# A three-layer block in split float32: all low parts subtracted on VectorE, none on GpSimd

## The chip, the cores and the metric

The kernel runs on one core of one Trainium2 chip. A core has five engines with instruction queues of their own: TensorE (PE, with weight loads shown apart as PEld), VectorE (DVE), ScalarE (ACT), GpSimd (POOL) and SyncE (SP), which here only issues transfers. The metric is the device time of one execution in microseconds (us); less is better.

## What is computed

512 tokens of 1024 features go through a first block and then a second one of two layers. Cut to what matters here:

```
first block:  h = x + mixing(norm(x))                 # state space, gated mixing, w_out
              h = h + experts(norm(h))                # 8 heads; each token picks 16 of 16384 experts per head:
                                                      #   sum over them of gate * gelu(norm(h) . U[e]) * V[e]
              h = h + sigmoid(norm(h) w_gate) * (p w_proj);  then a norm
second block: h = [16 meta tokens, h]
              layer 0: h += mixer_ab(norm(h));  h += relu(norm(h) w_ff1)^2 w_ff2
              layer 1: h += attention(norm(h)); h += relu(norm(h) w_ff1)^2 w_ff2
```

All of it is float32.

## The kernel before

A large product is made in three passes of the type float32r. Each operand is written as a high and a low part: `split` copies the source to the high part on ScalarE (line 288, which rounds to float32r) and then subtracts this from the source to give the low part (line 289). The passes are high by high, high by low and low by high (`product`, line 314); the pass with the low part of the weights comes last.

`weights` fetches one unit of 128 x 1024 weights, 512 KB, from HBM into a buffer `w_raw` by a transfer on SP's queue and splits it into `w_hi` and `w_lo`, of which there are two buffers each. `w_raw` has six buffers in the experts' part and two or three elsewhere. A unit feeds 24 matmuls, 16 with `w_hi` and 8 with `w_lo`. The argument `eng` of both functions names the engine that subtracts: VectorE where it is not given, GpSimd where it is.

The stages in order of time, with the place of GpSimd's subtractions:

- 0 to 280 us: `mix_layer`, with state space, gates and `w_out`. Six units of `w_in`, and two of `wq` at the start of `peer`.
- 280 to 300 us: the norm of the experts' input. For eight chunks of features, `hn` is split; the odd four on GpSimd.
- 300 to 600 us: `retrieve` searches the best experts of all tokens: per head, products with `wq` and with keys, then on VectorE `max`, `max_index` and `match_replace` (lines 1091 to 1095), and comparisons with the sums of pairs (lines 1147 to 1154). Beside it, `ahead` makes products of units of `U` that are needed later (70 in all, here and in the next stage), and keeps their gelu in HBM. Nearly all units are subtracted on GpSimd.
- 600 to 840 us: `scatter_gates` makes one-hot tiles of the chosen experts by comparisons on VectorE (line 1216), scales half of one on GpSimd (line 1217) and half on ScalarE, and multiplies them on TensorE into a table of gates. The other products of `ahead` go beside it, subtracted on GpSimd.
- to 1690 us: the dense experts, for the first 384 tokens. For each of 16 groups of 8 keys: the rest of the `U` products, gates times gelu (line 949), their split `ga`, and 8 products with units of `V` added to h (line 984). Here `less_loaded` chose VectorE or GpSimd for each unit by an account of the load of both, with 1.13 us for VectorE and 2.3 us (`W_POOL`) for GpSimd; `pace` adds to it what the row work costs.
- Beside the last three: `Own` gathers, for the last 128 tokens, rows of `U` and `V` by indirect transfers that GpSimd issues (line 1058), one row of 4 KB for each token at a time; VectorE multiplies each (line 1037) or adds it (line 1041). Four are under way at a time.
- 1690 to 1830 us: `per_layer`, then `delta_inputs` of the second block, whose twelve units of `w_ab` are subtracted on GpSimd.
- After 1830 us: the rest of the second block. VectorE makes all subtractions.

The order of instructions on each engine is not written out by hand: the framework plans it before the run from a timeline that it simulates (`schedule_with_timeline_sim=True`), starting from the order of the program. On the chip each engine takes its instructions in that order.

Of the kernel before, what the change touches and what calls it, by code (L numbers as in the profile page):

```python
# [11 lines left out]
F32 = mybir.dt.float32  # L12
# [34 lines left out]
def _rows(v):  # L47
    """A vector laid out along the free axis of all 128 partitions."""
    return _c(np.broadcast_to(np.asarray(v).reshape(1, -1), (128, np.asarray(v).size)))


def _feat(x):
    """[tokens, features] -> [128, chunks, tokens]."""
    return _c(x.T.reshape(-1, 128, x.shape[0]).transpose(1, 0, 2))


def _pairs(b):
    """[32 groups, 64 states, 16 channels] -> block diagonal over pairs of groups [128, 16, 32]."""
    out = np.zeros((2, 64, 16, 2, 16), b.dtype)
    b = b.reshape(16, 2, 64, 16)  # L60
    for g in range(2):
        out[g, :, :, g, :] = b[:, g].transpose(1, 0, 2)
    return out.reshape(128, 512)
# [10 lines left out]
def _half_cols(w):  # L74
    """The two members of every rotary pair into two halves of a head."""
# [110 lines left out]
class Ctx:  # L186
    """Pools and constants; tokens are `T` columns in `nb` PSUM banks of `hn` each."""
# [9 lines left out]
    def enter(self, name, side):  # L197
        """A pool that `leave` closes; once h is on the right, the sides are exchanged."""
# [13 lines left out]
    def psum(self, mm, aux):  # L212
        """PSUM as `mm` accumulators of all tokens and `aux` single banks."""
# [5 lines left out]
    def raw_units(self, n):  # L219
        """`n` buffers for units of weights, in an order that all that is loaded there keeps."""  # L220
# [5 lines left out]
    def work(self):  # L226
        """Pools of small tiles and of the tiles of norms."""
# [20 lines left out]
def newton_rsqrt(c, v, n):  # L248
    """1/sqrt(v) of a [128, n] tile, elementwise, to float32 accuracy."""
# [13 lines left out]
def exp_exact(c, out, x, n):  # L263
    """exp of a [128, n] tile to float32 accuracy."""
# [19 lines left out]
def split(c, src, hi, lo, scale=None, eng=None):  # L284
    """src (times a per-partition scale) as a sum of two float32r parts."""
    nc = c.nc
    if scale is None:
        nc.scalar.activation(hi, src, AF.Copy)  # L288
        (eng or nc.vector).tensor_tensor(lo, src, hi.bitcast(F32), ALU.subtract)  # L289
# [5 lines left out]
def weights(c, src, nk, n, eng=None):  # L295
    """Load one unit of weights and split it: two float32r views [128, nk, n]."""
# [5 lines left out]
    split(c, raw, hi, lo, eng=eng)  # L302
# [3 lines left out]
def product(c, ps, parts, first=True, last=True, n=None, late=1):  # L306
    """ps [M, nb, 512] += sum of stationary^T moving over three passes; moving holds all tokens (or one bank of n).
    The passes with the second part of the stationary (late=1) or moving (late=2) side come last."""
# [9 lines left out]
def token_stats(c, acc, width):  # L318
    """rsqrt(mean + eps) per token from partial sums acc [128, T]: [tokens of a tile, tiles]."""
# [15 lines left out]
def along_tokens(c, col):  # L335
    """A per-token column [128, tiles] as a row on all partitions: PSUM banks of `hn` tokens."""
# [15 lines left out]
def square_sum(c, acc, k, src, eng=None, scale=1.0):  # L352
    """acc += (src * scale) squared (the first chunk starts it)."""
# [9 lines left out]
def token_rows(c, acc, width, name):  # L363
    """rsqrt(mean + eps) as rows on all partitions, in SBUF, and as columns."""
# [4 lines left out]
def column_rows(c, col, name):  # L369
    """A per-token column as rows in SBUF."""  # L370
# [7 lines left out]
class Rows:  # L378
    """The rows of a norm, made when first asked for; uses of them wait until `hold` products are under way."""
# [20 lines left out]
class S5:  # L400
    """Powers of the discretised transition, the input and output weights of chunks of 4 tokens."""
# [74 lines left out]
    def scaled(self, dst, src, by, eng, name):  # L476
        """dst = src * by; parts along the second axis, `by` the real and the imaginary part and the negative of that."""
# [9 lines left out]
    def inputs(self, j):  # L487
        """The input weights of position j in a chunk; position 3 comes first."""
# [9 lines left out]
    def transposes(self):  # L498
        """The input weights as the stationary side of products."""
# [10 lines left out]
    def rotations(self, k):  # L510
        """The rotations of positions 2^k and more, after those before, of a chunk."""
# [11 lines left out]
    def powers(self):  # L523
        """The output weights of the state."""
# [17 lines left out]
    def inside(self, q):  # L542
        """The output weights of the chunk itself, of 4 pairs of groups."""
# [16 lines left out]
def s5_states(c, pool, xs, S, hf):  # L560
    """The states before each chunk, of 8 of the 16 pairs of groups; xs is [(position in chunk, channel), pair, chunk]."""
# [38 lines left out]
def s5_outputs(c, pool, xs, S, hf, h, ys):  # L600
    """ys = gelu of the outputs of these pairs."""
# [21 lines left out]
def mix_layer(c):  # L623
    """Block 1 up to the residual after w_out, which becomes c.h."""
    nc, d = c.nc, c.d
    tt = nc.vector.tensor_tensor
    with c.pool("mix", "right") as pool:
# [3 lines left out]
        with c.pool("s5", "right") as s5p:  # L631
# [3 lines left out]
            with c.pool("s5t", "right") as tmp:  # L635
                S = S5(c, s5p, outer, tmp)
                acc = c.norm("acc")
                for k in range(8):
                    x = pool.tile([128, 512], F32, name="u", bufs=5)
                    nc.sync.dma_start(x, d["xT"][:, k])  # L640
                    if k == 0:
                        w = weights(c, d["w_in"][0], 8, 128, eng=nc.gpsimd)
# [7 lines left out]
                for m in range(4):  # L650
                    ps = c.mm()
                    product(c, ps, [((w[0][:, k], w[1][:, k]), xk[k]) for k in range(8)])
                    if m < 3:
                        w = weights(c, d["w_in"][m + 1], 8, 128, eng=None if m else nc.gpsimd)
# [16 lines left out]
                for what, step in [(o[0], int(o[1])) for o in V_ORDER]:  # L671
                    if what == "v":
# [9 lines left out]
                        else:  # L682
                            w = weights(c, d["w_in"][4], 8, 128, eng=nc.gpsimd)
# [12 lines left out]
            for what, step in [(o[0], int(o[1])) for o in U_ORDER]:  # L696
                if what == "u":
                    ps = c.mm()
                    product(c, ps, [((w[0][:, k], w[1][:, k]), xk[k]) for k in range(8)])
                    if step < 3:  # L700
                        w = weights(c, d["w_in"][5 + step], 8, 128, eng=nc.gpsimd)
# [26 lines left out]
            def half(m, k0, pair):  # L728
                """Half of the product of output chunk m; weights come for two chunks at a time."""
# [60 lines left out]
def sgu_norm(c, vn, mean):  # L790
    """The norm of v [token, head, tile, channel] in place, from its sums over channels."""
# [14 lines left out]
def sgu_weights(c, pool):  # L806
    """The causal weights of the mixing, and what it adds."""
# [14 lines left out]
def sgu_mix(c, gp, u, vn, wb):  # L822
    """u *= causal mixing of the normalised v."""
# [21 lines left out]
PER_CALL = 0.6  # L845
# [6 lines left out]
PER_USE = 1.2  # L852
PER_FETCH = 1.04
W_POOL = 2.3


def peer(c, acc, hn):
    """Its norm goes to hn, and h += the retrieved experts, summed with their gates: all experts with the gates of the first 384 tokens,
    and for the last 128 tokens the rows of their own experts."""
# [3 lines left out]
    with c.pool_d("peer_d") as dram, c.pool("gel", "left") as gelp:  # L863
        rows = Own(c, gelp)
        w_q = [weights(c, d["wq"][k], 8, 128, eng=nc.gpsimd) for k in range(2)]
# [14 lines left out]
        for k in range(8):  # L880
            t = gelp.tile([128, 512], F32, name="gel", bufs=GEL)
            nc.vector.scalar_tensor_tensor(t, c.h[k], c.vec("g_ffn", k), row, op0=ALU.mult, op1=ALU.mult)
            split(c, t, hn[0][:, k], hn[1][:, k], eng=nc.gpsimd if k % 2 else None)
# [7 lines left out]
        def reach(a, eng):  # L891
            """gelu of the dense tokens against the 128 experts of key a: [expert, token]."""
            w = weights(c, d["U"][a], 8, 128, eng=eng)
# [6 lines left out]
        def ahead(k, eng):  # L900
            for _ in range(min(k, len(first) - len(early))):
                s = first[len(early)]
                early[s] = dram.tile([128, n], F32, name="early%d" % s)
                nc.sync.dma_start(early[s], reach(s, eng))

        place = lambda: gelp.tile([128, 512], F32, name="gel", bufs=GEL)
        load = [0.0, 0.0]

        def less_loaded():
            """The engine that ends a split of weights first."""  # L910
            k = 0 if load[0] + 1.13 <= load[1] + W_POOL else 1
            load[k] += (1.13, W_POOL)[k]
            return (nc.vector, nc.gpsimd)[k]

        with c.pool("sel", "right") as sel:
# [9 lines left out]
            def beside(i, n):  # L925
                ahead((i + 1) * rest // n - i * rest // n, nc.gpsimd)
# [4 lines left out]
        ahead(128, nc.gpsimd)  # L931

        with c.pool("ga", "right") as gp:
# [4 lines left out]
            def prepare(s, ga):  # L938
# [3 lines left out]
                else:  # L942
                    gel = reach(s, less_loaded())
# [14 lines left out]
            def pace(cost):  # L958
                """Rows in step with the work done, out by the last group."""
# [4 lines left out]
                load[0] += PER_USE * k + PER_CALL  # L964
                load[1] += PER_FETCH * k

# [3 lines left out]
            for g in range(16):  # L970
                if g < 15:
                    nxt = pair()
                for m in range(8):
# [5 lines left out]
                    w = weights(c, d["V"][8 * g + m], 8, 128, eng=less_loaded())  # L979
# [17 lines left out]
class Own:  # L997
    """The last 128 tokens, one per partition: rows of their experts, gathered in step with other work."""
# [19 lines left out]
    def choose(self, e16):  # L1018
        """The experts [128, 2, 16] of the next two heads."""
# [4 lines left out]
    def use(self, i, r, at=None):  # L1024
        """Row i times its weight, which passes through `at` of the work that this keeps step with."""
# [17 lines left out]
    def go(self, k, place):  # L1043
        """Fetch the next k rows; their numbers pass through a tile of the work that they keep step with."""
# [18 lines left out]
    def add(self):  # L1063
        """The rest of the rows; then their sum into h."""
# [13 lines left out]
def retrieve(c, tk, hk, rows, go, ahead, first):  # L1078
    """The experts and gates of all tokens, [token, tile, head, slot]; two heads at a time, with other work between.
    `first` holds products of the tokens before their norm, with its rows."""  # L1080
# [16 lines left out]
    def keys_of(h, s16, i16):  # L1097
        """The 16 best keys of both halves of head h."""
# [3 lines left out]
        for k in range(2):  # L1102
# [3 lines left out]
            w = weights(c, d["wq"][2 * h + k], 8, 128, eng=nc.gpsimd)  # L1106
# [16 lines left out]
    def pairs_of(h2, s16, i16):  # L1123
        """The 16 best pairs of heads h2 and h2 + 1; rows of tiles are (tile, head)."""
# [18 lines left out]
        for t in (3, 0, 1, 2):  # L1143
# [11 lines left out]
            ahead(1, nc.vector if t == 0 else nc.gpsimd)  # L1155
# [5 lines left out]
    for h2 in range(0, 10, 2):  # L1161
        now = new()
        if h2 < 8:
            keys_of(h2, *now)
            ahead(2, nc.gpsimd)
# [3 lines left out]
        if h2 < 8:  # L1169
            keys_of(h2 + 1, *now)  # L1170
            ahead(2, nc.gpsimd)
# [15 lines left out]
def by_slot(c, tk, e16, gate, s, at, bt, gt):  # L1187
    """The chosen pairs and gates of a token tile as [slot, token]."""
# [14 lines left out]
def scatter_gates(c, sp, at, bt, gt, g_all, beside):  # L1203
    """g_all[b, block, a, token] = summed gate of expert (a, b) for the dense token."""
# [25 lines left out]
def per_layer(c, acc, hg):  # L1230
    """h += sigmoid(norm(h) w_gate) * (p w_proj), and what the norm that ends the block and the next one need: the sums of
    squares of h and of h sqrt(g^2 + eps), h g itself in DRAM, and h g and the meta tokens times the next gain as float32r pairs,
# [1024 lines left out]
```

## Time and profile before

| | |
|---|---|
| median of 3 runs | 3222.72 us (3222.37 to 3227.86) |
| span of the profiled execution | 3231.5 us, 47250 instructions |
| its own time beside the span | not recorded; only the span is |
| TensorE matmuls | 2989.7 us busy, 93% |
| TensorE weight loads | 2704.9 us, 84% |
| VectorE | 2449.9 us, 76% |
| ScalarE | 1269.3 us, 39% |
| GpSimd | 1261.8 us, 39% |
| line 289, GpSimd, low parts of weights | 201 subtractions, 532.8 us |
| line 289, VectorE, low parts of weights | 297 subtractions, 409.2 us |

Busy time runs from an instruction's start to its end and so holds whatever it waits for once it has begun. A group's mean is over instructions that may have met different conditions; the least and the median of its durations tell them apart. Two neighbouring instructions of one engine overlap a little, so the distance of their starts, back to back, is what one costs.

### The profile page before, as it was taken

To read this page: it belongs to the slowest core of one execution; us is meant where nothing else is said; L and a number is where in the kernel's file an instruction comes from. 1 tells how busy PE (TensorE), PEld (TensorE's weight loads), DVE (VectorE), ACT (ScalarE), POOL (GpSimd) and SP (SyncE) were. 2 spreads that over 40 slices of the span, in tenths; PEclk is the share of its full clock that TensorE was granted. 3 is DMA by queue.
4 is the path that set the end of the run, shared out by engine and by line. 5 is a ranking of instruction groups with operands and counts; after the bars stand their busy time and mean duration, and the time that the engine had idled before them with its cause. 6 is when DMAs were issued, how large, how long until landed. Compare 5 with 4: busy or idle time off the path is not lost. (4 is left out here: it accounts for less than half of the span.)

```text
span 3231.5 us, 47250 instructions
## 1 busy us (share of the span) xinstructions
PE 2989.7 (93%) x17801; PEld 2704.9 (84%) x17801; DVE 2449.9 (76%) x4680; ACT 1269.3 (39%) x2170; POOL 1261.8 (39%) x786
## 2 busy tenths in 40 slices
PE   4878997899999999999999999899999999999999
PEld 3667997888999999899997899655999997778887
DVE  9977899999799999999998965664534446665352
ACT  3644332577633333333344433144323324443241
POOL 5335566787577677777754202011000012010000
PEclk8988998999999999999999999788999999999999
DMA  2213355566798899998952220011222221022232
GB/s 100 72 53 108 133 170 183 189 229 243 246 311 301 307 305 317 315 311 303 314 198 83 71 73 9 1 47 36 88 92 92 92 86 46 24 79 92 97 98 91
DMA packets 202888, 485.06 MB, mean 150 GB/s; under 512 B 25676, under 2 KB 95780, under 8 KB 199588
## 3 DMA queue, kind: packets, MB, share of 16 engines
q1 hardware_dynamic: 165796, 347.81, 32.3%
q0 software_dynamic: 36864, 134.23, 12.0%
q8 instruction: 140, 2.29, 0.3%
q14 instruction: 88, 0.72, 0.1%
HBM read 437.42 MB, written 44.55 MB: 149 GB/s over the span
## 5 line engine op out<-in xcount | busy, mean ns | idle before, releaser
L288 ACT ACTIVATE w_hi<-w_raw 128x1024 fp32r<-128x1024 f32 (+1 forms) x498 | 511.4, 1028 | 750.7 <-PE mm L314 627.2
L289 POOL TENSOR_TENSOR w_lo<-w_raw,w_hi 128x1024 fp32r<-128x1024 f32 x201 | 532.8, 2653 | 206.5 <-ACT w_hi L288 112.0
L289 DVE TENSOR_TENSOR w_lo<-w_raw,w_hi 128x1024 fp32r<-128x1024 f32 (+1 forms) x297 | 409.2, 1378 | 138.2 <-ACT w_hi L288 96.5
L314 PE MATMUL mm<-hn,w_hi 128*128 128x384 f32 (+1 forms) x2400 | 486.4, 351 | 1.8 <-DVE hn L289 1.3
L314 PEld LDWEIGHTS mm<-hn,w_hi 128*128 128x128 f32 x2400 | 429.0, 191 | 17.8 <-DVE hn L289 1.6
L314 PE MATMUL mm<-ga,w_hi 128*128 128x384 f32 x2048 | 389.6, 343 | 5.5 <-DVE ga L289 3.7
L314 PEld LDWEIGHTS mm<-ga,w_hi 128*128 128x128 f32 x2048 | 368.9, 193 | 8.0 <-DVE ga L289 5.1
L314 PE MATMUL mm<-xg,w_hi 128*128 128x264 f32 (+1 forms) x1920 | 345.9, 334 | 20.5 <-ACT w_hi L288 8.8
L360 POOL TENSOR_TENSOR acc<-acc,sq 128x512 f32<-128x512 f32 (+1 forms) x55 | 86.1, 1570 | 658.7 <-ACT sq L359 654.4
L314 PEld LDWEIGHTS mm<-xg,w_hi 128*128 128x128 f32 x1920 | 290.0, 191 | 59.2 <-DVE xg L292 12.4
L314 PE MATMUL mm<-hn,w_lo 128*128 128x384 f32 (+1 forms) x1200 | 259.1, 353 | 13.7 <-POOL w_lo L289 6.4
L314 PE MATMUL mm<-hid,w_hi 128*128 128x264 f32 (+1 forms) x1536 | 251.1, 319 | 0.0
L1058 POOL DMA_INDIRECT own_row<-V_rows,f x128 | 204.9, 1601 | 92.2 <-DVE f L1034 52.1
L314 PEld LDWEIGHTS mm<-hid,w_hi 128*128 128x128 f32 x1536 | 223.0, 188 | 20.0
L314 PEld LDWEIGHTS mm<-hn,w_lo 128*128 128x128 f32 x1200 | 214.8, 191 | 25.8 <-DVE w_lo L289 9.3
L314 PE MATMUL mm<-ga,w_lo 128*128 128x384 f32 x1024 | 207.3, 345 | 30.8 <-DVE w_lo L289 20.6
L288 ACT ACTIVATE ga<-f 128x384 fp32r<-128x384 f32 x128 | 67.0, 525 | 378.3 <-DVE f L949 370.9
L314 PEld LDWEIGHTS mm<-ga,w_lo 128*128 128x128 f32 x1024 | 182.5, 192 | 38.9 <-DVE w_lo L289 24.2
L1041 DVE SCALAR_TENSOR_TENSOR own_x<-own_row,f,own_x 128x1024 f32<-128x1024 f32 x123 | 195.6, 1590 | 0.5
L314 PE MATMUL mm<-xg,w_lo 128*128 128x264 f32 (+1 forms) x960 | 173.6, 329 | 0.0
L1058 POOL DMA_INDIRECT own_row<-U_rows,f x87 | 129.1, 1484 | 83.5 <-DVE f L1034 64.5
L314 PEld LDWEIGHTS mm<-xg,w_lo 128*128 128x128 f32 x960 | 144.9, 188 | 17.1
(732 smaller groups left out, 5357.2 us busy)
## 6 DMA issues: line engine op xcount, KB each, us to landing
w_raw<-U SPq DMA_DIRECT2D x128, 512.0 KB
w_raw<-V SPq DMA_DIRECT2D x128, 512.0 KB
w_raw<-w_f SPq DMA_DIRECT2D x128, 512.0 KB
g_all<-stage SPq DMA_DIRECT2D x24, 1024.0 KB
g<-g_all SPq DMA_DIRECT2D x32, 768.0 KB
early<-gel SPq DMA_DIRECT2D x70, 192.0 KB
gel<-early SPq DMA_DIRECT2D x70, 192.0 KB
w_raw<-w_ab SPq DMA_DIRECT2D x22, 512.0 KB
```

The costliest lines, as they stand in the source:

```text
L288: nc.scalar.activation(hi, src, AF.Copy)
L289: (eng or nc.vector).tensor_tensor(lo, src, hi.bitcast(F32), ALU.subtract)
L314: c.nc.tensor.matmul(ps[:, h, :hn], lhsT=st[a], rhs=mv[b][:, h * hn:(h + 1) * hn], start=first and i == 0, stop=last and i == len(order) - 1)
L360: (eng or nc.gpsimd).tensor_tensor(acc, acc, sq, ALU.add)
L1041: stt(self.acc, r, weight, self.acc, op0=ALU.mult, op1=ALU.add)
L1058: nc.gpsimd.indirect_dma_start(out=r, out_offset=None, in_=self.c.d["U_rows" if i0 < 128 else "V_rows"], in_offset=bass.IndirectOffsetOnAx ...
```

## The change

All splits are subtracted on VectorE. `split` and `weights` lose the argument `eng`, and all calls that named GpSimd lose it too: the units of `w_in`, `wq`, `U` and `w_ab`, the four odd chunks of `hn`, and the units of the dense experts, where the account of the load goes with its constants. The doc strings are taken out as well, which leaves the program as it is. The number of buffers, the transfers, the products and all other work of GpSimd stay.

```diff
-def split(c, src, hi, lo, scale=None, eng=None):
+def split(c, src, hi, lo, scale=None):
     nc = c.nc
     if scale is None:
         nc.scalar.activation(hi, src, AF.Copy)
-        (eng or nc.vector).tensor_tensor(lo, src, hi.bitcast(F32), ALU.subtract)
+        nc.vector.tensor_tensor(lo, src, hi.bitcast(F32), ALU.subtract)
...
-def weights(c, src, nk, n, eng=None):
+def weights(c, src, nk, n):
...
-    split(c, raw, hi, lo, eng=eng)
+    split(c, raw, hi, lo)
...
-                        w = weights(c, d["w_in"][m + 1], 8, 128, eng=None if m else nc.gpsimd)
+                        w = weights(c, d["w_in"][m + 1], 8, 128)
...
-            split(c, t, hn[0][:, k], hn[1][:, k], eng=nc.gpsimd if k % 2 else None)
+            split(c, t, hn[0][:, k], hn[1][:, k])
...
-        def reach(a, eng):
+        def reach(a):
-            w = weights(c, d["U"][a], 8, 128, eng=eng)
+            w = weights(c, d["U"][a], 8, 128)
...
-        load = [0.0, 0.0]
-
-        def less_loaded():
-            k = 0 if load[0] + 1.13 <= load[1] + W_POOL else 1
-            load[k] += (1.13, W_POOL)[k]
-            return (nc.vector, nc.gpsimd)[k]
-
...
-                    gel = reach(s, less_loaded())
+                    gel = reach(s)
...
-                load[0] += PER_USE * k + PER_CALL
-                load[1] += PER_FETCH * k
...
-                    w = weights(c, d["V"][8 * g + m], 8, 128, eng=less_loaded())
+                    w = weights(c, d["V"][8 * g + m], 8, 128)
...
-            w = weights(c, d["wq"][2 * h + k], 8, 128, eng=nc.gpsimd)
+            w = weights(c, d["wq"][2 * h + k], 8, 128)
...
-            ahead(1, nc.vector if t == 0 else nc.gpsimd)
+            ahead(1)
...
-    load = lambda m: weights(c, d["w_ab"][m], 8, 128, eng=nc.gpsimd)
+    load = lambda m: weights(c, d["w_ab"][m], 8, 128)
```

## Rows read from the trace of the kernel before

**Rows 1.** Page: busy us, share and instructions; then 40 slices in tenths.
```profile
PE 2989.7 (93%) x17801; PEld 2704.9 (84%) x17801; DVE 2449.9 (76%) x4680; ACT 1269.3 (39%) x2170; POOL 1261.8 (39%) x786
...
DVE  9977899999799999999998965664534446665352
...
POOL 5335566787577677777754202011000012010000
```

**Rows 2.** Stretches: length, busy us (instructions) of PE PEld DVE ACT POOL, clock, DMA share, GB/s.
```profile
300.00:500.00 200.00, 200.00 (x1072) 184.60 (x1071) 166.63 (x673) 71.32 (x94) 116.59 (x86) 1.00 0.46 151
500.00:600.00 100.00, 76.99 (x394) 74.73 (x392) 99.45 (x226) 27.40 (x39) 66.30 (x43) 0.88 0.62 193
600.00:840.00 240.00, 220.51 (x1411) 207.20 (x1412) 238.49 (x271) 184.62 (x331) 188.51 (x139) 0.99 0.63 226
...
900.00:1600.00 700.00, 663.07 (x3680) 651.23 (x3681) 684.84 (x1025) 231.42 (x309) 524.00 (x281) 0.98 0.90 309
```

**Rows 3.** The same stretches, line 289 alone: DVE busy (x), POOL busy (x), clock, DMA.
```profile
0.00:280.00 280.00, 25.66 (x20) 27.38 (x10) 0.88 0.23 77
...
300.00:500.00 200.00, 3.62 (x3) 95.37 (x37) 1.00 0.46 151
500.00:600.00 100.00, 1.20 (x1) 38.72 (x16) 0.88 0.62 193
600.00:840.00 240.00, 3.67 (x3) 78.54 (x26) 0.99 0.63 226
...
900.00:1600.00 700.00, 238.53 (x178) 220.90 (x86) 0.98 0.90 309
1600.00:1690.00 90.00, 24.67 (x22) 21.58 (x8) 0.96 0.68 232
1690.00:1830.00 140.00, 13.37 (x9) 29.31 (x11) 0.95 0.24 78
```

**Rows 4.** Timeline near 1307 us: start, duration, engine, instruction [idle before <- releaser].
```profile
1306.94 3.92 DVE L289 TENSOR_TENSOR w_lo<-w_raw,w_hi 128x1024 fp32r<-128x1024 f32 x1
1307.37 2.40 POOL L289 TENSOR_TENSOR w_lo<-w_raw,w_hi 128x1024 fp32r<-128x1024 f32 x1
...
1309.82 1.65 PE L314 MATMUL mm<-ga,w_lo 128*128 128x384 f32 x8 [0.62 <-POOL w_lo L289]
```

**Rows 5.** Instructions by tile or line, 900 to 1600: durations in ns, least/median/most.
```profile
L289 POOL TENSOR_TENSOR w_lo<-w_raw,w_hi x86: 2357/2416/3408, 906.9 to 1596.0; 128x1024 fp32r<-128x1024 f32 x86
L289 DVE TENSOR_TENSOR w_lo<-w_raw,w_hi x68: 1207/1217/3974, 896.2 to 1594.0; 128x1024 fp32r<-128x1024 f32 x68
...
L984 DVE TENSOR_TENSOR h<-mm,h x109: 539/550/558, 901.0 to 1596.8; 128x384 f32<-128x384 f32 x109
```

**Rows 6.** Timeline near 986 us, DVE back to back.
```profile
985.71 1.21 DVE L289 TENSOR_TENSOR w_lo<-w_raw,w_hi 128x1024 fp32r<-128x1024 f32 x1
...
986.85 0.54 DVE L949 TENSOR_TENSOR f<-gel,g 128x384 f32<-128x384 f32 x1
```

**Rows 7.** Stretches of 20 us in which TensorE has no gap, columns as in rows 2.
```profile
1020.00:1040.00 20.00, 20.00 (x118) 20.00 (x117) 19.83 (x31) 6.19 (x9) 14.94 (x8) 1.00 0.88 297
...
840.00:860.00 20.00, 20.00 (x131) 20.00 (x130) 9.11 (x11) 13.87 (x22) 7.24 (x6) 1.00 0.60 208
```

**Rows 8.** Groups, 300 to 500, then 500 to 600: busy us, mean ns | idle before <- releaser.
```profile
L1153 DVE TENSOR_TENSOR hit<-hit,expert 128x1600 f32<-128x1600 f32 x11 | 31.4, 2853 | 0.1
L1149 DVE TENSOR_TENSOR hit<-posf,iota 128x1600 f32<-128x1600 f32 x11 | 19.9, 1810 | 0.1
...
L1091 DVE MAX8 s<-sc 128x8 f32<-128x128 f32 x48 | 11.4, 279 | 33.1 <-ACT sc L1118 33.1
...
L1037 DVE SCALAR_TENSOR_TENSOR own_row<-own_row,gel,own_x 128x1024 f32<-128x1024 f32 x13 | 35.2, 2713 | 0.0
...
L1037 DVE SCALAR_TENSOR_TENSOR own_row<-own_row,gel,own_x x13: 1264/1752/6390, 512.9 to 590.1; 128x1024 f32<-128x1024 f32 x13
```

**Rows 9.** Groups with the idle time before them: 2300 to 2640, then 300 to 600.
```profile
L289 DVE TENSOR_TENSOR w_lo<-w_raw,w_hi 128x1024 fp32r<-128x1024 f32 x59 | 71.9, 1218 | 49.2 <-ACT w_hi L288 28.3 <-PE mm L314 20.9
...
L289 POOL TENSOR_TENSOR w_lo<-w_raw,w_hi 128x1024 fp32r<-128x1024 f32 x52 | 134.1, 2582 | 61.9 <-PE mm L314 35.0 <-ACT sc L1118 14.8 <-ACT w_hi L288 11.7
```

More of the change, by code (lines that the diff above doesn't have):

```diff
@@ L641, in mix_layer @@
                     if k == 0:
-                        w = weights(c, d["w_in"][0], 8, 128, eng=nc.gpsimd)
+                        w = weights(c, d["w_in"][0], 8, 128)
                     split(c, x, xg[0][:, k], xg[1][:, k], scale=c.vec("g_mix", k))
@@ L682, in mix_layer @@
                         else:
-                            w = weights(c, d["w_in"][4], 8, 128, eng=nc.gpsimd)
+                            w = weights(c, d["w_in"][4], 8, 128)
                     elif what == "b":
@@ L700, in mix_layer @@
                     if step < 3:
-                        w = weights(c, d["w_in"][5 + step], 8, 128, eng=nc.gpsimd)
+                        w = weights(c, d["w_in"][5 + step], 8, 128)
                     u.append(pool.tile([128, 512], F32, name="u", bufs=5))
@@ L844 @@
 G_ROWS = 28
-PER_CALL = 0.6
 GEL = 4
@@ L851 @@
 GEL2 = 2
-PER_USE = 1.2
-PER_FETCH = 1.04
-W_POOL = 2.3
 def peer(c, acc, hn):
@@ L864, in peer @@
         rows = Own(c, gelp)
-        w_q = [weights(c, d["wq"][k], 8, 128, eng=nc.gpsimd) for k in range(2)]
+        w_q = [weights(c, d["wq"][k], 8, 128) for k in range(2)]
         low = [c.raw(F32R) for _ in range(4)]
@@ L898, in reach, with ahead @@
             return gel
-        def ahead(k, eng):
+        def ahead(k):
             for _ in range(min(k, len(first) - len(early))):
@@ L903, in ahead @@
                 early[s] = dram.tile([128, n], F32, name="early%d" % s)
-                nc.sync.dma_start(early[s], reach(s, eng))
+                nc.sync.dma_start(early[s], reach(s))
         place = lambda: gelp.tile([128, 512], F32, name="gel", bufs=GEL)
-        load = [0.0, 0.0]
-        def less_loaded():
-            k = 0 if load[0] + 1.13 <= load[1] + W_POOL else 1
-            load[k] += (1.13, W_POOL)[k]
-            return (nc.vector, nc.gpsimd)[k]
         with c.pool("sel", "right") as sel:
@@ L925, in beside @@
             def beside(i, n):
-                ahead((i + 1) * rest // n - i * rest // n, nc.gpsimd)
+                ahead((i + 1) * rest // n - i * rest // n)
                 rows.go((i + 1) * G_ROWS // n - i * G_ROWS // n, place)
@@ L930, in peer @@
                 scatter_gates(c, sp, at, bt, gt, g_all, beside)
-        ahead(128, nc.gpsimd)
+        ahead(128)
         with c.pool("ga", "right") as gp:
@@ L1164, in retrieve @@
             keys_of(h2, *now)
-            ahead(2, nc.gpsimd)
+            ahead(2)
         if before:
@@ L1170, in retrieve @@
             keys_of(h2 + 1, *now)
-            ahead(2, nc.gpsimd)
+            ahead(2)
             go(GO_H)
@@ L1320 @@
 class Delta:
+    pass
 def delta_inputs(c, keep, pool, xk, rows):
```

## The prediction

> **What bounds the kernel now.** I read the busy table and the slices first [rows 1]: the reader is to see that VectorE (DVE) is at seven tenths or more, mostly nine, through the first 57% of the span and idle by halves afterwards, while GpSimd (POOL) works only in that first part. A change that puts POOL's subtractions on DVE therefore meets DVE where it looks full. The table by stage [rows 2] shows where: the search for the best experts (300 to 600 us), the scatter of the gates (600 to 840) and the dense experts (900 to 1600). From 300 to 500 TensorE is busy without a gap and DVE has 33 us free; from 500 on DVE is at 98 to 99% and TensorE has gaps. So from 500 to 840 and from 900 to 1600 DVE sets the pace, and the question is what DVE's busy time is made of.
>
> The third view counts the subtractions of line 289 by stage [rows 3]. POOL makes 37, 16, 26 and 86 of them in the stages named, 10 and 11 in the two stages around (0 to 280, 1690 to 1830), and 201 in all, besides four of half the length for hn.
>
> The timeline tells what they do to DVE [rows 4]. A DVE subtraction shown from 1306.94 lasts 3.92 us; a POOL subtraction runs from 1307.37 to 1309.77, and DVE's ends 1.09 us after it. TensorE, which needed POOL's result, starts at 1309.82. So one engine's busy time was the other's run: the two did not work side by side. The lists of durations say the same [rows 5]: the DVE subtraction has a median of 1217 ns and a maximum of 3974, while the addition that reads one input from PSUM (line 984) never leaves 539 to 558 ns. The operations held are those that read SBUF twice, like most of DVE's work here. DVE's 98% is therefore partly waiting for POOL.
>
> The Trainium skill (SBUF — State Buffer, section "SBUF: two separate sides") has a rule for this: VectorE and GpSimd arbitrate for one pair of ports by an exclusive lock, and whichever starts first keeps it for its whole instruction. In the rows DVE stands first and still ends last, so the trace agrees on the hold but not on who wins; by the rule as written POOL would wait in half of the meetings, and dense DVE relief would be about half of what follows.
>
> **The change, part by part.** Removed from POOL: 201 subtractions of 2.42 us (median) [rows 5]. Added to DVE: the same 201. Back to back, DVE takes 1.14 us for one (985.71 to the next start at 986.85) [rows 6]. What a POOL subtraction takes from DVE is bounded by nothing (no DVE operation needs the ports) and by its whole run, some 2.3 us. Which end applies is read by stage. The planner's accounting (less_loaded, load) costs no time itself.
>
> *Dense experts, 900 to 1600.* DVE's busy time is 684.8 us with 86 POOL subtractions in it [rows 2, 3]. The meeting of [rows 4] held DVE for 3.92 - 1.22 = 2.70 us, POOL's median is 2.42 [rows 5]; I take 2.26 for each, an estimate a little under both, since DVE at times has something to do without the ports. That is 194 us of waiting. Moved, they cost 86 x 1.14 = 98 us. DVE's need goes from 685 to 685 - 194 + 98 = 589 us of 700. At the other end, no waiting to be had back, it would be 685 + 98 = 783, 83 us past the stage. I take the first: DVE is then busy 589, or 84%, and no longer the bound. What is late next is TensorE: undisturbed it gets through 118 matmuls in 20 us [rows 7], and it made 3680 in this stage [rows 2], so it needs 3680/118 x 20 = 624 us. The gap is 76 us. DMA stands in the way too: its engines are busy 0.90 of the stage [rows 2], so at a share of 1 the same bytes would want 630 us, a gap of 70. With TensorE at 624, DMA at 630 and DVE at 589 none of them will run without gaps; I take half of 72, so 36 us off.
>
> By TensorE's own busy time the gap would be only 700 - 663 = 37 us [rows 2]. The Trainium skill (Perfetto Trace Analysis, section "Identifying the Most-Contended Engine") says that matmul busy time misleads because matmuls are pipelined, and to go by weight-load busy time; that gives 700 - 651 = 49 us, and half of it 24. The count of matmuls gives more than either, and I go by the count.
>
> *Scatter, 600 to 840.* DVE is busy 238.5 of 240 us, with 26 POOL subtractions [rows 2, 3]. By the same step 238.5 - 26 x 2.26 + 26 x 1.14 = 209 us, 29 less. TensorE made 1411 matmuls; in the first 20 us after this stage, where DVE leaves it alone, it makes 131 [rows 7], so it needs 215 us: 25 us can be had. Against it, POOL's multiplications of the one-hot tiles stay and go on holding DVE. Half again: 12 us off. The bounds are 25 off and, without relief, 26 x 1.14 = 30 on.
>
> *Search, 300 to 600.* Here much of DVE's work (MAX8, FIND_INDEX8 and the like) reads one tile and runs beside POOL, so the relief is smaller. From 300 to 500 the product with the expert numbers (line 1153) averages 2.85 us, while its twin of the same shape (line 1149) takes 1.81 [rows 8]: 11 x 1.04 = 11 us to be had back, against 37 x 1.14 = 42 on. The net 31 us fits the 33 us for which DVE waits for scores [rows 8], but only just, and not all of that idle time lies where the subtractions come; TensorE is the bound there, and I put the loss at 6 us (bounds 0 and 31). From 500 to 600, 13 row products average 2.71 us where the quickest takes 1.26 [rows 8]: 19 us back from these alone, up to 16 x 2.26 = 36 from all, against 16 x 1.14 = 18. I take 12 us off (bounds 1 on, 18 off). Together 6 off.
>
> *The rest.* 21 subtractions from 0 to 280 and 1690 to 1830 cost 24 us on DVE and free up to 47; both stages have waits of TensorE, DVE and ScalarE in turn. I take 1 off (bounds 24 on, 23 off), the four hn pieces included. After 1830 there is one subtraction; nothing changes.
>
> Buffers: a w_raw buffer is free once both parts are made, so its next load is issued earlier; POOL's queue then holds only gathers, one-hot products and sums, and the gathers no longer stand behind a subtraction. Now the one-hot comparisons, row products and gate products on DVE are queued behind a subtraction that waits for ScalarE's w_hi.
>
> The sum: 36 + 12 + 6 + 1 = 55 us off. The rows come from a profiled execution with a span of 3231.5 us; what lies around the span is not shown, and the median of the unprofiled runs is 3222.7, 0.3% less, so I carry the difference over unscaled: 3222.7 - 55 = 3168 us.
>
> **The rivals.** *Transfers cap the dense stage.* For it: the DMA share of 0.90 in the mean of 700 us [rows 2]; against: in the full-speed slice it was 0.88 [rows 7]. The stage gives 10 us in place of 36, scatter and search 11: 3222.7 - 21 = 3202 us.
>
> *All gaps close.* 72 in the dense stage, 25 in scatter, 13 in search, 2 elsewhere: 112 us, 3111 us. For it: DVE at 84%; against: three engines within 7% of each other.
>
> *The subtraction waits in DVE's queue (slower).* DVE takes its instructions in order; a subtraction there must wait for w_hi, which waits for TensorE to give up a buffer, and everything behind it waits too. For it: in the feed-forward layer DVE stands idle 49.2 us before 59 subtractions, 0.83 us each, and in the search POOL stood 61.9 us before 52, 1.19 each [rows 9]. Against: where DVE is the late one, w_hi is long ready. At a wait w the 53 of the search cost 53 x (1.14 + w) less 30 back and 33 of idle time, and each of the 120 from 600 to 840 and 900 to 1690 [rows 3] gains 2.26 - 1.14 - w. That turns to a loss at w = 0.79 us: 53 x 1.93 - 63 = 39 lost, 120 x 0.33 = 40 gained. At 1.19 it is 53 x 2.33 - 63 = 60 lost and 120 x 0.07 = 8 more: 68 slower, 3291 us.
>
> *It moves the wait and no more.* The order on each engine is planned anew; TensorE's waits for a low part come back behind other DVE work: within 0.2%.
>
> **How the numbers follow.** Forecast 44%, transfers 20%, all gaps 12%, queue 17%, no change 7%. Within 0.2% (6.4 us) this kernel's measurement can't tell from no change. Faster 0.76, same 0.07, slower 0.17. The forecast's own range is 3145 to 3190; to hold 8 in 10 I go down to 3110 (all gaps) and up to 3250, well into the queue's case.
>
> **What would show it.** Right: from 900 to the end of the dense stage DVE's share falls to some 85 to 90% with subtractions near 1.2 us in the mean, row and gate products at their medians, the matmul count per 100 us goes from 526 to about 555, the DMA share rises to 0.95; POOL's busy time falls by 541 us to about 720, DVE's falls below 2400 although it has 201 operations more. Wrong: DVE idle before its subtractions with ScalarE's w_hi as the releaser and the search longer than 300 us (queue); or DVE's busy time up by some 230 us (no hold to be had back).

## The result, and the profile after

The changed kernel takes 3115.41 us (median of 4 runs, 3109.71 to 3124.9) against 3222.55 us (median of 4 runs, one more than ahead of the prediction): a ratio of 0.9677, 95% interval 0.9655 to 0.9699, or 107 us less. The time lies in the range (3110 to 3250), but outside the forecast's own 3145 to 3190; the rival "all gaps close" (3111) was nearer than the forecast (3168).

The profiled execution ended at 3107.8 us where that of before ended at 3231.5 [rows 1], 124 us earlier; the 17 us more than the medians' difference come from these two single executions: the span of before lies 9 us above its median, that of after 8 us below. The first lines are the page of after, as rows 1; then its group of all subtractions of weights.

```profile
PE 2933.5 (94%) x17801; PEld 2674.5 (86%) x17801; DVE 2300.4 (74%) x4885; ACT 1276.0 (41%) x2170; POOL 690.8 (22%) x581
...
DVE  9987999999789899999989755755525456764352
...
POOL 4241013365333334333321011001000021010000
...
L289 DVE TENSOR_TENSOR w_lo<-w_raw,w_hi 128x1024 fp32r<-128x1024 f32 (+1 forms) x498 | 596.6, 1200 | 154.0 <-ACT w_hi L288 98.3
```

VectorE has 205 instructions more and is busy 149.5 us less. GpSimd's busy time fell by 571 us.

The table by stage, as rows 2:

```profile
300.00:500.00 200.00, 200.00 (x1087) 186.50 (x1086) 188.26 (x715) 72.33 (x95) 30.95 (x55) 1.00 0.47 155
500.00:600.00 100.00, 100.00 (x571) 99.90 (x570) 96.03 (x235) 39.88 (x54) 38.67 (x29) 1.00 0.82 274
600.00:840.00 240.00, 213.26 (x1415) 206.21 (x1414) 215.28 (x315) 193.96 (x352) 121.20 (x111) 0.96 0.64 229
...
900.00:1500.00 600.00, 595.00 (x3413) 593.03 (x3412) 547.30 (x1025) 220.05 (x287) 237.15 (x182) 1.00 0.95 336
```

From 500 to 600 TensorE made 571 matmuls where it had made 394, and the mean granted clock went from 0.88 to 1.00, which is the upper of its two levels (2.4 GHz) for the whole stretch. In the dense experts it is busy 99% of the time. The dense stage ends at 1582, where it had ended at 1683.

The durations in the dense stage, 900 to 1500 (ns, least/median/most), beside rows 5; the first line is the gate product before, from 900 to 1600. Line numbers after the edit are 12 to 14 lower: 937 was 949, 1044 was 1058.

```profile
L949 DVE TENSOR_TENSOR f<-gel,g x108: 542/549/5619, 904.0 to 1592.9; 128x384 f32<-128x384 f32 x108
...
L289 DVE TENSOR_TENSOR w_lo<-w_raw,w_hi x143: 1207/1216/1227, 900.3 to 1497.3; 128x1024 fp32r<-128x1024 f32 x143
...
L937 DVE TENSOR_TENSOR f<-gel,g x101: 543/551/574, 903.1 to 1496.2; 128x384 f32<-128x384 f32 x101
...
L1044 POOL DMA_INDIRECT own_row<-V_rows,f x114: 935/1014/3549, 1129.9 to 1499.9; - x114
```

The reader is to look at the third figure. The subtraction's longest was 3974 ns and is 1227; the gate product's was 5619 and is 574. Both now stay within 25 ns of their medians, so nothing holds them in this stretch any more.

Landmarks of the timeline give the stages; the lengths add up to the two spans, but for rounding:

| stage, by landmarks | before | after | difference | forecast |
|---|---|---|---|---|
| 0 to the first `hn` | 286.6 | 277.1 | -9.5 | in "rest" |
| search, to the first one-hot tile | 312.2 | 333.1 | +20.9 | -6 |
| scatter, to the last one-hot tile | 247.6 | 199.1 | -48.5 | -12 |
| dense experts, to the last addition to h | 836.6 | 772.8 | -63.8 | -36 |
| to the first `qT` | 116.8 | 104.2 | -12.6 | -1, with the first line |
| to the end | 1431.7 | 1421.6 | -10.1 | 0 |

The last line holds five of GpSimd's former subtractions, all in its first 315 us, which got 1.9 us shorter; 7 of its 10 us lie in one stretch without any, 168 us long, in which the granted clock was 0.94 instead of 0.88. I don't count it to the change.

### The profile page after: what moved, and what is told of

It reads as the page before. It is cut to its first block, busy times and chain, and to the rows that moved or that the text cites. A ratio compares the mean times of both kernels' runs of the same rounds, so it can differ in the third digit from the quotient of the medians.

```text
span 3107.8 us, 47300 instructions
## 1 busy us (share of the span) xinstructions
PE 2933.5 (94%) x17801; PEld 2674.5 (86%) x17801; DVE 2300.4 (74%) x4885; ACT 1276.0 (41%) x2170; POOL 690.8 (22%) x581
## 3 DMA queue, kind: packets, MB, share of 16 engines
q0 software_dynamic: 36864, 134.23, 12.4%
## 5 line engine op out<-in xcount | busy, mean ns | idle before, releaser
L289 DVE TENSOR_TENSOR w_lo<-w_raw,w_hi 128x1024 fp32r<-128x1024 f32 (+1 forms) x498 | 596.6, 1200 | 154.0 <-ACT w_hi L288 98.3
L314 PE MATMUL mm<-ga,w_hi 128*128 128x384 f32 x2048 | 380.0, 336 | 3.3 <-DVE ga L289 3.3
L314 PEld LDWEIGHTS mm<-ga,w_hi 128*128 128x128 f32 x2048 | 357.6, 188 | 3.7 <-DVE ga L289 3.6
L314 PE MATMUL mm<-hn,w_lo 128*128 128x384 f32 (+1 forms) x1200 | 248.4, 347 | 0.0
L1044 POOL DMA_INDIRECT own_row<-V_rows,f x128 | 165.0, 1289 | 255.1 <-DVE f L1020 149.6
L314 PE MATMUL mm<-ga,w_lo 128*128 128x384 f32 x1024 | 199.9, 337 | 0.8 <-DVE w_lo L289 0.8
L1044 POOL DMA_INDIRECT own_row<-U_rows,f x87 | 114.6, 1317 | 203.8 <-DVE f L1020 155.3
L1027 DVE SCALAR_TENSOR_TENSOR own_x<-own_row,f,own_x 128x1024 f32<-128x1024 f32 x123 | 157.2, 1278 | 0.1
L314 PE MATMUL mm<-hid,w_lo 128*128 128x264 f32 (+1 forms) x768 | 130.5, 319 | 0.0
```

The lines of the kernel that those rows point to most:

```text
L289: nc.vector.tensor_tensor(lo, src, hi.bitcast(F32), ALU.subtract)
L314: c.nc.tensor.matmul(ps[:, h, :hn], lhsT=st[a], rhs=mv[b][:, h * hn:(h + 1) * hn], start=first and i == 0, stop=last and i == len(order) - 1)
L1027: stt(self.acc, r, weight, self.acc, op0=ALU.mult, op1=ALU.add)
L1044: nc.gpsimd.indirect_dma_start(out=r, out_offset=None, in_=self.c.d["U_rows" if i0 < 128 else "V_rows"], in_offset=bass.IndirectOffsetOnAx ...
```

## The experiments

The theory (H, "hold"): a subtraction on GpSimd held VectorE for most of its run, and taking it away gave that time back. The rival (O, "order"): the new order and the freed buffers did it, and GpSimd's work beside VectorE costs little. The framework plans the order of all engines anew for every kernel here, so no two of them differ in one thing alone.

### Parts of the change alone

On the kernel before, GpSimd's subtractions are moved in the dense experts only; in the search, scatter and `hn` only; and in `w_in`, the first two units of `wq` and `w_ab` only.

```diff
+            return nc.vector                     # in less_loaded: dense only
...
-                ahead(2, nc.gpsimd)
+                ahead(2, nc.vector)              # and likewise: search and scatter only
...
-    load = lambda m: weights(c, d["w_ab"][m], 8, 128, eng=nc.gpsimd)
+    load = lambda m: weights(c, d["w_ab"][m], 8, 128)   # and w_in: others only
```

> The kernel before, with only the dense experts' units all subtracted on VectorE (less_loaded always names it); search, scatter and the other stages keep GpSimd's subtractions. Theory H: the dense stage loses its 100 holds and runs at TensorE's pace: some 50 to 75 us less than before, 3148 to 3172. Rival O with the units pulled forward as the source of the gain: search and scatter are as before, so the dense stage still has as many units as before and gains little: 3200 to 3222.

> The kernel before, with only the units that are made in search and scatter (wq, the 70 of U made ahead) and the four hn pieces subtracted on VectorE. Theory H: search plus scatter together some 28 us shorter and a dozen units pulled forward, so that the dense stage is shorter by some 20 too, if it is not bound by VectorE: in all 28 to 50 us less, 3172 to 3195. Rival (VectorE's queue is the limit there): 3222 or slower.

> The kernel before, with only the twenty-odd subtractions from 0 to 280 us (w_in, the first two wq) and in the second block's first projections (w_ab) moved to VectorE. Theory H: the two stages, 10 and 13 us shorter in the changed kernel's profile, are shorter here too: 3200 to 3212. Rival (those differences belong to the profiles compared and not to the subtractions, as the dense part alone took 59 us and search and scatter alone 44, together all but a few us of the whole): within 5 us of the kernel before.

Measured: 3166.05 us, ratio 0.9829 (0.9807 to 0.985); 3180.76, 0.9877 (0.9854 to 0.99); 3208.17, 0.9958 (0.994 to 0.9976). That is 59, 44 and 14 us off. The three ratios lose 3.36% together and the whole change 3.23%, so the parts add within their intervals. The dense stage of the first, then search, scatter and dense stage of the second (columns as rows 2):

```profile
845.00:1621.00 776.00, 774.69 (x4416) 773.35 (x4416) 693.17 (x1278) 294.55 (x387) 296.92 (x223) 1.00 0.92 322
```

```profile
282.00:614.00 332.00, 330.73 (x1814) 315.09 (x1815) 311.81 (x1052) 125.63 (x169) 73.02 (x86) 0.99 0.57 190
614.00:816.00 202.00, 189.59 (x1285) 182.25 (x1283) 196.32 (x258) 178.13 (x325) 122.90 (x110) 1.00 0.62 226
816.00:1638.00 822.00, 771.51 (x4300) 758.49 (x4301) 775.05 (x1176) 281.34 (x381) 587.65 (x321) 0.98 0.88 301
```

With only its own subtractions moved, the dense stage takes 776 us instead of 836.6 for the same number of matmuls, and TensorE has 1.3 us of gaps in it. Its pace is 4416 matmuls in 776 us, 113.8 in 20 us. Where GpSimd keeps them, 50 us of gaps are left in 822. There search and scatter take 534 us instead of 559.8 and make 114 matmuls more; the dense stage makes 113 fewer and is 15 us shorter.

### Subtractions put back on GpSimd

On the changed kernel, each unit of the dense experts gets a subtraction on GpSimd whose result nobody uses. VectorE still makes all low parts.

```diff
     split(c, raw, hi, lo)
+    if junk is not None:         # a tile of 128x512, two of them in turn
+        nc.gpsimd.tensor_tensor(junk, raw[:, :512], raw[:, 512:], ALU.subtract)
```

> The changed kernel, and in the dense experts GpSimd makes, for each of the 186 units, a subtraction of one half of the raw weights from the other half (128x512, two inputs) into a spare tile that nobody reads. VectorE keeps all its subtractions. Theory H (a GpSimd operation with two SBUF inputs holds VectorE for its run): 186 x about 1.2 us = 220 us of holding meet a VectorE that is busy 688 of 773 us, so the stage grows by some 110 to 150 us, the time is 3225 to 3265, and VectorE's row products and gate products show long tails again while TensorE's records thin out. Rival O (the gain comes from the new planned order and from GpSimd's queue being short; there is no hold): GpSimd has 480 us free in the stage and nobody waits for the result, so 3115 within 15 us.

Measured: 3270.48 us, 1.0148 (1.0121 to 1.0176): 155 us lost of the changed kernel's time, a little beyond the range of H. The spare subtraction reads `w_raw`, though, so it also keeps the buffer (from 900 to 1500 the loads of weights waited 1.1 us for it). The next kernel takes this away: the operand is one element for each partition that ScalarE has copied, read 511 times, and the buffer is free without GpSimd.

```diff
+        nc.scalar.activation(junk[:, 0:1], raw[:, 0:1], AF.Copy)
+        one, rest = junk[:, 0:1].to_broadcast([128, 511]), junk[:, 1:512]
+        nc.gpsimd.tensor_tensor(rest, one, one, ALU.subtract)
```

> As the run with GpSimd's spare subtractions, but free of the raw weights: for each of the 186 units ScalarE copies one column of the raw unit into a spare tile, and GpSimd subtracts this column, spread over 511 places, from itself into the rest of that tile (128x511, two inputs, 1.3 us). No buffer of weights waits for GpSimd. Theory H: VectorE is held for 186 x 1.2 us or somewhat less, 3215 to 3265. Rival O, or the raw buffers as the cause of the loss in the first form: 3115 to 3130.

Measured: 3238.19 us, 1.0048 (1.0031 to 1.0066), as H has it; O falls. The stretch, the durations, the groups and the waits of SP's queue from 900 to 1500, then the timeline at two meetings:

```profile
900.00:1500.00 600.00, 541.47 (x2946) 525.13 (x2945) 567.79 (x897) 202.46 (x370) 396.18 (x280) 0.97 0.87 290
...
L943 DVE TENSOR_TENSOR f<-gel,g x86: 542/547/2901, 911.9 to 1498.2; 128x384 f32<-128x384 f32 x86
...
L306 POOL TENSOR_TENSOR sq<-sq 128x511 f32<-128x511 f32 x122 | 167.4, 1377 | 61.8 <-ACT sq L304 60.2 <-issue 0.2
L289 DVE TENSOR_TENSOR w_lo<-w_raw,w_hi 128x1024 fp32r<-128x1024 f32 x123 | 182.5, 1489 | 0.8 <-issue 0.8
...
SPq L299 <- DVE w_lo L289: 300.3, 101, 9.1
...
SPq L299 <- ACT sq L304: 0.4, 2, 0.2
...
1102.38 1.18 POOL L306 TENSOR_TENSOR sq<-sq 128x511 f32<-128x511 f32 x1
1102.59 1.38 DVE L943 TENSOR_TENSOR f<-gel,g 128x384 f32<-128x384 f32 x1
...
1109.03 2.63 DVE L943 TENSOR_TENSOR f<-gel,g 128x384 f32<-128x384 f32 x1 [0.65 <-DMA own_row<-U_rows,f]
1109.20 2.03 POOL L306 TENSOR_TENSOR sq<-sq 128x511 f32<-128x511 f32 x2
```

VectorE made 128 instructions fewer than after in the same 600 us and was busy 20 us more. At after's mean of 547.30/1025 = 0.534 us the 897 would have taken 479; the other 89, over 122 spare subtractions, are 0.73 us held by each, an estimate, where the quickest of them takes 1.03. The gate product ends some 0.4 us after GpSimd's operation, both where GpSimd began first and where VectorE did. No kept buffer explains the loss: the loads of weights waited for VectorE's low parts (300.3 us, and 291.5 after), 0.4 us for ScalarE's small copy and not for GpSimd.

### Copies in their place

The same two kernels with two copies on GpSimd, which have one input, instead of the subtraction were to tell whether any work there holds VectorE.

```diff
+        for half in (raw[:, :512], raw[:, 512:]):
+            nc.gpsimd.tensor_copy(junk, half)
...
+        for _ in range(2):                # second kernel, operand as above
+            nc.gpsimd.tensor_copy(rest, one)
```

> As the run before it, but in place of the subtraction GpSimd copies the two halves of the raw weights one after the other (372 copies of 128x512, one input each). If only GpSimd operations that read two inputs hold VectorE: 3115 to 3130. If every GpSimd operation that works on SBUF holds it: a copy should last 0.5 to 0.7 us, 186 to 260 us in all, and the time is 3200 to 3265, as with the subtractions. Rival O: 3115 within 15 us in both runs.

> As the run before it, with two copies of the column over the 511 places (one input each, some 0.6 us) in place of one subtraction, so that GpSimd is busy for as long. If only operations with two inputs hold VectorE: 3115 to 3135. If any GpSimd operation on SBUF does: 3200 to 3265. If the 3364 of the first form with copies came from GpSimd keeping the raw buffers, as its trace says (loads waited 174 us for GpSimd's copies), this one is well below that in either case.

Measured: 3363.73 us, 1.0436 (1.0412 to 1.0459), and 3433.65, 1.0652 (1.0628 to 1.0676). Neither theory had that, so the times don't tell the two apart. The waits of SP's queue and of ScalarE in the first kernel, then the same in the second (total, times, longest), with its stretch:

```profile
SPq L299 <- POOL sq L305: 173.8, 54, 11.5
...
ACT w_hi L288 <- DMA w_raw<-V: 104.9, 37, 8.7
```

```profile
SPq L299 <- ACT sq L304: 283.6, 62, 14.1
...
ACT w_hi L288 <- DMA w_raw<-V: 126.7, 40, 8.8
...
900.00:1500.00 600.00, 489.62 (x2501) 472.97 (x2501) 448.70 (x780) 168.41 (x306) 397.67 (x324) 0.91 0.73 244
```

In both the loads of weights were late, because a buffer was kept: in the first by GpSimd's copies, in the second by ScalarE's small copy. VectorE was idle a quarter of the second stretch. What the times can't tell of the hold, the durations do (second kernel, 900 to 1500: gate product, addition from PSUM, and one meeting):

```profile
L944 DVE TENSOR_TENSOR f<-gel,g x75: 540/559/964, 900.2 to 1498.8; 128x384 f32<-128x384 f32 x75
...
L977 DVE TENSOR_TENSOR h<-mm,h x74: 539/547/559, 904.6 to 1489.0; 128x384 f32<-128x384 f32 x74
...
906.66 0.96 DVE L944 TENSOR_TENSOR f<-gel,g 128x384 f32<-128x384 f32 x1
...
907.12 0.97 POOL L307 COPY sq<-sq 128x511 f32<-128x511 f32 x1
```

Of the 75 gate products 36 met a copy, with a median of 0.96 us; the others took 0.56 us at most, and so did the addition from PSUM. So a one-input operation of GpSimd holds VectorE's two-input ones too, here by up to 0.4 us. What that alone costs the kernel stays open.

### More work taken from GpSimd

If two-input work on GpSimd holds VectorE, the rest of it should pay as well. On the changed kernel: the scaling of the one-hot tiles moved to VectorE; the running sums of squares of the norms moved; these and the state space's products; these and all the other two-input work of the layers but the scaling of the one-hot tiles and the sums of candidate pairs.

```diff
-            nc.gpsimd.tensor_tensor(hot[:, 1, ON_ACT:], hot[:, 1, ON_ACT:],
+            nc.vector.tensor_tensor(hot[:, 1, ON_ACT:], hot[:, 1, ON_ACT:],
...
-        (eng or nc.gpsimd).tensor_tensor(acc, acc, sq, ALU.add)
+        (eng or nc.vector).tensor_tensor(acc, acc, sq, ALU.add)
```

> The changed kernel, and the scaling of half of each one-hot tile in the scatter (line 1203, 96 operations of 128x256 with two inputs) also on VectorE. Theory H: each of them on GpSimd still holds VectorE by 0.42 us (the second comparison's median is 1.10 us in place of 0.68); on VectorE each costs 0.35 to 0.4 us; and ScalarE is at 94% in the second half of the stage: so no gain worth the name, 3105 to 3120. Rival (GpSimd's work is free as long as it is short): VectorE's work grows by 96 x 0.6, the stage by up to 30 us: 3140.

> The changed kernel, and all sums of squares (line 360, 55 additions of two tiles of 128x512 on GpSimd, 87 us) also on VectorE. Theory H: where VectorE is the late one (14 of them before 277 us) each frees up to 1.6 us and costs 0.6, so up to 14 us; elsewhere VectorE has room: 3100 to 3112 against 3115 of the changed kernel. Rival (GpSimd's additions run where VectorE does not need the ports): 3115 to 3125.

> As the run before it, and the state space's GpSimd work of two inputs (powers, its skip term, and the four sums and products of each half, some 55 us before 250 us) on VectorE. Theory H: VectorE is busy 241 of 277 us before the experts' part, some of it held; moving 55 us of GpSimd's work costs VectorE 25 to 30 us and frees up to 55, so up to 25 us more off if it is held throughout, nothing if half of GpSimd's work meets VectorE's own one-input work: 3085 to 3112. Rival: those of GpSimd's operations run beside VectorE's small ones, and VectorE's chain grows by what it is given: up to 25 us slower than the run before it.

> As the run before it, and GpSimd's two-input work of the second block (rotations, decayed queries, the levels' masks, the residual of w_out) on VectorE too; GpSimd keeps the gathers, the scaling of one-hot tiles and the sums of candidate pairs. Theory H: VectorE is at 50 to 70% there and the chain changes between engines, so within 8 us of the run before it, either way. Rival (GpSimd's share is worth having where VectorE is not the late one): 10 to 20 us slower.

Measured: 3125.12 us, 0.9719 (0.9682 to 0.9756), no gain over the change and 5 us above what H had; 3090.39, 0.9607 (0.9586 to 0.9629); 3094.3, 0.9611 (0.9591 to 0.963); 3087.34, 0.9593 (0.9577 to 0.9608). The sums of squares gained about 0.7% more than the change, 10 us beyond the end of what was expected; what was added to them after that can't be told from nothing. The last kernel beats both before and after; its interval overlaps with that of the sums of squares alone. With the one-hot tiles TensorE waited for ScalarE's half (next section), and giving VectorE the other half did not help that: in this stage it then waited 5.1 us for ScalarE's and 8.0 for VectorE's. Why the sums of squares gained so much was not taken apart: the profile has the first `hn` 10 us earlier than after and the feed-forward layer begins 20 us earlier.

## Why the prediction was right, and where its sizes were off

The range holds the result because its lower end was set by *all gaps close*; the forecast's own sum, 55 us, is about half of the 107 measured. The mechanism was right, and the sizes of what TensorE would make of it were not.

**The hold is what was given back: right.** I took 2.26 us for each meeting and so 589 us of VectorE for the 3680 matmuls of the dense stretch. After, 547.30 us went with 3413, which scales to 547.30 x 3680/3413 = 590. The trace shows the hold itself: in the dense stretch VectorE's operations ran 205 us, in sum, beyond the shortest of their kind (same line, tiles and shape) before and 9 us after, so some 2.3 us for each of the 86 subtractions. From 300 to 600 it was 59 and 11 us (48 given back, forecast 11 and 30), from 600 to 840 96 and 36 (60, forecast 59).

The Trainium skill (SBUF — State Buffer, "SBUF: two separate sides") says that VectorE operations in a two-port mode, and those with two SBUF inputs against a GpSimd operation that reads SBUF, take turns with GpSimd, and that the first to start wins. The first half agrees with the runs: two-input operations fell to their medians, and the addition from PSUM was never longer than 558 ns [rows 5]. The second does not fit the recorded starts: at 1109.03 VectorE stood first and ended last, and so did 34 of the 83 operations of VectorE that met a subtraction of GpSimd from 900 to 1600 before and took over 0.3 us more than the shortest of their kind.

One reading of the prediction was too narrow, that the operations held are those that read SBUF twice. The cast of the positions, with one input, was held too, each time beside a subtraction of GpSimd (before, then after; the same line of the program); whether it runs in a two-port mode no run shows:

```profile
L1147 DVE CAST posf<-pos x16: 165/387/2228, 349.6 to 576.5; 128x32 f32<-128x32 uint32 x16
...
L1133 DVE CAST posf<-pos x16: 166/172/179, 343.6 to 581.3; 128x32 f32<-128x32 uint32 x16
```

**The dense term: 36 forecast, 59 alone.** The step that failed is "I take half of 72". TensorE, the DMA engines (0.95) and VectorE (0.91) do run side by side here with hardly a gap; no allowance was due for three engines within some per cent of each other. The gap itself was over-sized: 118 matmuls in 20 us came from one good stretch [rows 7], and the undisturbed pace is 113.8. So the 3680 needed 647 us and the gap was 53, not 76. All of 53 over a stage of 836.6 us is 53 x 836.6/700 = 63; alone it gave 60.6 by the profile. By the weight loads' busy time, as the Trainium skill has it (Perfetto Trace Analysis, "Identifying the Most-Contended Engine"), the gap was 49, nearer than my count. TensorE's busy time gave 37, too little: one matmul's share of it fell too, from 663.07/3680 = 0.180 us to 595.00/3413 = 0.174, while the mean granted clock went from 0.98 to 1.00.

**Search and scatter: 18 forecast, 44 alone.** The hold was sized about right: the product with the expert numbers fell to its twin, as forecast, and the row products nearly to their least [rows 8]. What TensorE made of it was mis-sized, twice. After, from 300 to 600, and then TensorE's longest wait before, from 500 to 600:

```profile
L1023 DVE SCALAR_TENSOR_TENSOR own_row<-own_row,gel,own_x 128x1024 f32<-128x1024 f32 x24 | 30.5, 1276 | 0.0
L1139 DVE TENSOR_TENSOR hit<-hit,expert 128x1600 f32<-128x1600 f32 x16 | 29.1, 1817 | 0.0
L1135 DVE TENSOR_TENSOR hit<-posf,iota 128x1600 f32<-128x1600 f32 x16 | 29.1, 1816 | 0.0
...
L289 DVE TENSOR_TENSOR w_lo<-w_raw,w_hi 128x1024 fp32r<-128x1024 f32 x64 | 77.8, 1215 | 7.6 <-DMA w_raw<-U 3.4 <-issue 1.5 <-PE mm L314 1.4
...
PE aux L1191 <- DVE posf L1147: 12.4, 2, 8.0
```

From 500 to 600 the 23 us in which TensorE stood idle [rows 2] are gone, not the 12 I took; in 12.4 of them it had waited for VectorE. (The lower bound of that term has its sign wrong: 19 back against 18 is 1 off, not 1 on.) The search got 20.9 us longer, which the forecast did not have; it is not the loss the queue rival told of, since it made 292 matmuls more (1821, was 1529) and scatter 179 fewer. I had capped scatter by its old count of matmuls, and the planner changed the count. Both stages together are 27.6 us shorter with 113 matmuls more, which the dense stage need not make: at 113.8 in 20 us another 20, so 47 in all. TensorE still waits in scatter, for ScalarE's half of the one-hot tiles (11.1 us in 27 waits).

**The rest: 1 forecast, 14 alone.** I bounded it by 24 on and 23 off and took the middle. The 14 lie between, and which operations gave them stays open. Moved alone, these subtractions bring the first `hn` forward by 6.5 us and make the stage up to the first `qT` 12 us shorter. The middle left out that GpSimd holds chains of tiny VectorE operations in the norms, each of which waits for the one before. The timeline of before, near 275 us:

```profile
274.60 0.16 DVE L259 SCALAR_TENSOR_TENSOR rs_y<-rs_a,rs_y 128x4 f32<-128x4 f32 x1
274.72 4.68 POOL L289 TENSOR_TENSOR w_lo<-w_raw,w_hi 128x1024 fp32r<-128x1024 f32 x2 [8.77 <-ACT w_hi L288]
274.80 2.30 DVE L257 SCALAR_TENSOR_TENSOR rs_a<-rs_y,ts_v 128x4 f32<-128x4 f32 x1
277.13 2.28 DVE L258 TENSOR_TENSOR rs_a<-rs_a,rs_y 128x4 f32<-128x4 f32 x1
...
280.08 1.19 PE L346 MATMUL aux<-sq,ones 128*128 128x128 f32 x4 [4.24 <-DVE sq L341]
```

An operation on 128x4 takes 0.16 us; two took 2.3 us each, one beside each of GpSimd's two subtractions, and TensorE waited 4.24 us for the end of the chain. That wait is not what was gained, though. After the change, and then with the rest moved alone, it reads:

```profile
PE aux L346 <- DVE sq L341: 4.5, 1, 4.5
```

```profile
PE aux L346 <- DVE sq L341: 6.5, 1, 6.5
```

After the change two of VectorE's own subtractions stand in the chain; with the rest moved alone, two of GpSimd's still run beside it.

**The rivals.** *Transfers cap the dense stage* fell: the share rose to 0.95 and 336 GB/s. *The queue* fell: in the search VectorE stood idle 7.6 us before 64 subtractions, 0.12 each, where 0.79 was the turning point; in the dense stage 9.9 before 143. *It moves the wait* fell: TensorE's waits for low parts of weights in the dense stretch were 31.6 us before and 0.8 after (before from 900 to 1600, then after from 900 to 1500):

```profile
PE mm L314 <- DVE w_lo L289: 19.0, 10, 2.7
PE mm L314 <- POOL w_lo L289: 12.6, 15, 1.7
```

```profile
PE mm L314 <- DVE ga L289: 3.3, 1, 3.3
...
PE mm L314 <- DVE w_lo L289: 0.8, 2, 0.6
```

*All gaps close* (112 us) is what happened, though its own terms were off too: 72 dense against 59, 38 search and scatter against 44, 2 elsewhere against 14.

Of what was to show it, the matmul count per 100 us came to 569 (3413 in 600 us) where 555 stood, VectorE's share to 91% where 85 to 90 stood, and GpSimd's busy time to 690.8 where 720 stood.

## What to carry to other kernels

Before an elementwise operation goes to GpSimd to relieve VectorE, compare the least, the median and the longest duration of VectorE's own operations beside such work: where the longest is above the median by GpSimd's run, the two take turns. Here a subtraction on GpSimd took some 2.3 us from VectorE, which makes it itself in 1.14. Look at tiny VectorE operations too, as they are held as long as large ones. And when a held engine is freed, size the stage by what the next engine needs for its count of work, at a pace averaged over a whole stretch, and expect the gap to close.

## What was not expected of the hardware

The length of a VectorE operation does not matter for the hold: 128x4 took 2.3 us instead of 0.16 beside a subtraction of 128x1024. A copy on GpSimd, with one input, holds as well. An operation that begins first can still be the one that waits (2.63 us for one with a median of 0.55, begun 0.17 us before GpSimd's). GpSimd's issue of a gather got shorter as well, from a median of 1755 ns before to 1014, with no subtraction near it; the cause was not looked for.
